# A hybrid SSD, short-convolution and mixture-of-experts block on one core: a changed gather of the second token block, a sort in another place, and changed first and last stages

## The chip, the core and the metric

The kernel runs on one core of a Trainium2 chip. Five engines work side by side, each through its own instructions in order: TensorE (PE, its weight loads PEld), VectorE (DVE), ScalarE (ACT), GpSimd (POOL) and SyncE (SP), which here issues nearly all DMAs. The metric is the device time of one execution in microseconds; the kernel before takes 448.89 us (median of 3 runs, 448.59 to 450.16).

## What is computed

One block of a decoder over 16 meta tokens and 256 tokens of width 1024, all in float32:

```python
u = rmsnorm(h, norm_mix)
proj = u @ w_in                                   # 1024 x 6160
y_ssd = ssd_branch(...)                           # Mamba-2 chunked scan
y_sc  = short_conv_branch(...)                    # gated short convolution
h = h + concatenate([y_ssd, y_sc]) @ w_out        # 2048 x 1024
u2 = rmsnorm(h, norm_ffn)
h = h + hier_moe(u2, ...)                         # 4 groups x 4 experts: best group, best 2 in it
return rmsnorm(h, norm_final)[:, N_META:]

def hier_moe(...):
    for e in range(16):
        out = out + combine[:, e:e + 1] * ((silu(t @ w_gate[e]) * (t @ w_up[e])) @ w_down[e])
```

`combine` is zero for all but two experts of a token, so only routed rows have to be multiplied.

## The kernel before

**Staging.** The order of the work is written out by hand: every engine runs its instructions in the order of the code. The weights stream through a ring of 22 slots of 1 MB (three more late in the program): `load` issues a slot's DMA on SP when the slot's last user is done, 24 tiles of `w_in`, 8 of `w_out`, 96 of the experts. The small parameter DMAs stand in a list `between`; `load` issues three of them after each piece of the first weight tiles (L95 to L97). SP's DMAs use eight completion semaphores in turn, so a DMA's issue waits for the DMA eight before it.

**The start (L697 to L730).** Tokens come in two blocks b of 128. Each is normalised: ACT sums squares (`u_squares`, in halves of 512), DVE scales by the root and by `norm_mix` (`u_scale`, L247), which a DMA has copied to all 128 partitions (`gmix`, L173); PE turns it (`u_turn`, L279) into `uh`, its low part goes to `ul`. `x_part` (L271) multiplies the identity by x, which puts the residual x into the four PSUM accumulators `acc[b][n]`. Then 48 units of 128 output columns are projected (L337, `p_dt`, `p_B`, `p_C`, ...): ACT and DVE or POOL split a weight tile into a high and a low part (`split_hi` L313, `split_lo` L324), and PE makes three products of eight matmuls.

**The routing (L900 to L974).** For each block: h out of the accumulators, its root (`h_scale`, L801), router logits, places of each token in its experts (`places`, `ranks`, `pick`). `gather` (L891) picks the tokens of unit 0, the first two experts, by multiplying h (float32) by a 0/1 matrix P into `xp`, block 0 and then block 1, and DVE scales this to `X` (`rows`, L1078). `sort_experts` (L868 to L886, 15 small DVE operations) orders the ten experts from number 6 on by their counts and leaves `order` and the largest count `mosti`.

**The experts (L1179 on).** Seven units: six of two experts with 64 token places each, and a last one of four with 32. Each: gate and up products (`gu`, L1038), the places' transposes and weights (`back`, `ptp`), the next unit's tokens from three bf16 parts of h, `hparts` (`gather3`, L1111; the parts are made at L1096 to L1104), `turned`, the down product (`yd`) in two halves of 512 columns, and the weighted sum back into the accumulators (`weighed`, `scatter` L1059). Ahead of the units stands

```python
rv = nc.values_load(mosti[0:1], min_val=0, max_val=2 * S)      # L1172
```

which every engine runs as a TENSOR_LOAD at that place of its queue (for the branch at L1292); SP also loads `order`, for the addresses of the experts from number 6 on.

**The end (L1193 to L1202, L1241 to L1290).** During the last unit `norm_final` is spread over the partitions with a diagonal matrix and `fin_part` (L1066). The last unit's result goes to the accumulators in parts, and `last_norm` squares, takes roots, scales and writes out.

Of the kernel before, what the change touches and what calls it, by code (L numbers as in the profile page):

```python
# [25 lines left out]
HALVES = [(0, 512), (512, 512)]  # L26
DUM = 5
# [11 lines left out]
def body(ctx, tc, x, meta_tokens, norm_mix, w_in, ssd_conv_w, ssd_conv_b, dt_bias, A_log, D_skip,  # L39
# [95 lines left out]
    fcol = cp.tile([128, KT], F32, name="fcol")  # L135
# [17 lines left out]
    gmix = sA[:, 0:1024]  # L153
# [32 lines left out]
    between += [(dtb[:16], raw(dt_bias, 0, [[1, 16], [1, 1]])), (alog, raw(A_log, 0, [[0, 128], [1, 16]])),
                (dsk, raw(D_skip, 0, [[1, 2], [2, 8]])), (gf, raw(norm_ffn, 0, [[KT, 128], [1, KT]])),
                (fcol, raw(norm_final, 0, [[KT, 128], [1, KT]])),
# [11 lines left out]
    A.activation(warm, eps, AF.Sqrt)  # L200
    G.iota(half[:2], pattern=[[1, 128]], base=64, channel_multiplier=-64, allow_small_or_imprecise_dtypes=True)
# [4 lines left out]
    V.memset(zero, 0.0)  # L206
# [16 lines left out]
    sup = bp.tile([128, 128], BF, name="sup")
    V.tensor_scalar(sup, jp, 0.0, None, op0=OP.is_gt)
# [6 lines left out]

    def u_squares(b):
        un[b] = un01[:, 1024 * b:1024 * b + 1024]
        for n in range(2):
            c = slice(512 * n, 512 * n + 512)
            A.activation(un[b][:, c], xt[:, b, c], AF.Square, accum_out=norms[:, 3 * n + b:3 * n + b + 1])

    def u_root(b):
        rr[b] = r = norms[:, b:b + 1]
        V.tensor_scalar(r, r, 1.0 / D, EPS, op0=OP.mult, op1=OP.add)  # L240
        A.activation(r, norms[:, 3 + b:4 + b], AF.Sqrt, bias=r, scale=1.0 / D)
# [459 lines left out]
    V.tensor_copy(f0, zero.to_broadcast([128, 2048]))  # L701
    V.tensor_add(stack, idt[:32, 0:16], idt[:32, 16:32])
# [12 lines left out]
    u_root(1)  # L715
    for q in range(2):
        t[0, q] = u_turn(0, q)
    x_part(1, 0)
# [12 lines left out]
    for i, (name, j, c, t0) in enumerate(units):  # L731
# [105 lines left out]
    def ranks(b):  # L837
# [50 lines left out]
    def gather(b, q, p, i0=0, i1=4):  # L888

        for i in range(i0, i1):  # L890
            T.matmul(p[:, i], hh[:, b].rearrange("p (m k) -> p k m", k=KT)[:, 4 * q + i],  # L891
                     P[:, b], start=(b == 0 and i == 0), stop=(b == 1),
                     skip_group_check=True)
# [57 lines left out]
    P = bp.tile([128, 2, 128], F32, name="P")  # L951
# [19 lines left out]
    sort_experts(rp[:, 96:112])  # L971
    for q in range(2):
        gather(1, q, xp[q])
# [88 lines left out]
    def fin_part(q, tag):  # L1062

        p = bank(tag, "fp")
        for i in range(4):
            T.matmul(p[:, 128 * i:128 * i + 128], on1, dg[:, 4 * q + i], start=True, stop=True)  # L1066
        V.tensor_copy(fin.rearrange("p (m k) -> p k m", k=KT)[:, 4 * q:4 * q + 4],
                      p.rearrange("p (k m) -> p k m", k=4))

# [11 lines left out]
    h3 = wk.tile([128, 2, D], BF, name="h3")  # L1081
# [11 lines left out]
    hb0, hb1 = (hh[:, b].bitcast(BF).rearrange("p (j d) -> p j d", j=2) for b in range(2))
    hparts = [[h3[:, 0], hb0[:, 0]], [h3[:, 1], hb0[:, 1]], [hb1[:, 0], hb1[:, 1]]]
    rem = [wk.tile([128, 512], F32R, name="rem", tag=t).bitcast(BF) for t in ("Yh", "Yl")]
    for b in range(2):  # L1096
        A.activation(hparts[0][b], hh[:, b], AF.Copy)
        if b == 0:
            A.activation(ws0, eps, AF.Silu)
        V.tensor_tensor(hh[:, b], hh[:, b], hparts[0][b], op=OP.subtract)  # L1100
        A.activation(hparts[1][b], hh[:, b], AF.Copy)
        V.tensor_tensor(rem[b], hh[:, b], hparts[1][b], op=OP.subtract)
    for b in range(2):
        A.activation(hparts[2][b], rem[b], AF.Copy)  # L1104
# [74 lines left out]
    for u, ne in enumerate(UNITS):  # L1179
        last = u == len(UNITS) - 1  # L1180
        Xf = X.rearrange("p k t -> p (k t)")
        for kind in range(2):
# [7 lines left out]
            if kind == 0:  # L1190
                hb = wk.tile([128, 512], F32, name="hb", tag="Yh")
                A.activation(hb, g, AF.Silu)  # L1192
                if last:  # L1193
                    ff = slot("fin", free.pop(0))
                    dg, fin = ff[:, 0:1024].rearrange("p (k m) -> p k m", k=KT), ff[:, 1024:2048]
                    oo = slot("o", free.pop(0)).rearrange("p (b d) -> p b d", b=2)
                    on1 = oo[:, 0, 0:128]
                    V.memset(on1, 1.0)
                    V.tensor_tensor(dg, idt[:, None].to_broadcast([128, KT, 128]),
                                    fcol[:, :, None].to_broadcast([128, KT, 128]), op=OP.mult)  # L1200
                    left[1, 1] = [lambda: fin_part(0, "pj")]
                    left[1, 3] = [lambda: fin_part(1, "m")]  # L1202
# [11 lines left out]
        if not last:  # L1214
# [26 lines left out]
    Y0 = [wk.tile([128, 512], F32R, name=n, tag=n) for n in ("Yh", "Yl")]  # L1241
    Y1 = ff[:, 0:512]
    A.activation(Y0[0], ys[0], AF.Copy, scale=ws)
    V.scalar_tensor_tensor(Y0[1], ys[0], ws, Y0[0].bitcast(F32), op0=OP.mult, op1=OP.subtract)
    for n in range(2):
        A.activation(Y1[:, 256 * n:256 * n + 256], ys[1][:, 256 * n:256 * n + 256], AF.Copy, scale=ws)
    for b in range(2):
        scatter(b, 0, PT, Y0[0:1])
    for b in range(2):
        for c in range(2):  # L1250
            T.matmul(acc[b][1][:, 256 * c:256 * c + 256], PT.bitcast(F32)[:, 128 * b:128 * (b + 1)],
                     Y1[:, 256 * c:256 * c + 256], start=False, stop=True, skip_group_check=True)
            if b == 0:
                scatter(c, 0, PT, Y0[1:], True)

    def norm_part(b, c0, w):
        c = slice(c0, c0 + w)
        V.scalar_tensor_tensor(oo[:, b, c], acc[b][c0 // 512][:, c0 % 512:c0 % 512 + w], s3[:, b:b + 1], fin[:, c],
                               op0=OP.mult, op1=OP.mult)
        (A if c0 == 512 else nc.sync).dma_start(raw(out, b * 128 * D + c0, [[D, 128], [1, w]]), oo[:, b, c])  # L1260

    def squares_of(b, n):
        A.activation(oo[:, b, 512 * n:512 * n + 512], acc[b][n], AF.Square, accum_out=s4[:, b, n:n + 1])
# [7 lines left out]
    def last_norm():  # L1271
        squares_of(0, 0)
        first_sum(0)
        squares_of(0, 1)
        root(0)
        V.reciprocal(s3[:, 0:1], s3[:, 0:1])
        for n in range(2):
            squares_of(1, n)

        norm_part(0, 0, 256)  # L1280
        first_sum(1)
        root(1)
# [35 lines left out]
```

## Time and profile before

| what | us |
|---|---|
| median of 3 runs (range) | 448.89 (448.59 to 450.16) |
| the profiled execution | 448.21 |
| its span in the trace | 446.2 |
| PE, DVE, ACT, POOL busy | 422.9, 229.9, 159.4, 66.2 |
| DMA: bytes moved, mean rate | 139.85 MB, 313 GB/s |

The span is what the trace covers, and 2.0 us of the profiled time lie around it. Busy time of PE counts pipelined matmuls by modelled ends, so where an engine waits says more than its share. A chain of waits is read from the last instruction backwards: each piece is what released the next.

### The profile page before, as it was taken

The numbers are of one execution on the slowest core, as the hardware profiler recorded it, in microseconds if no ns is written. First come the engines' busy times: TensorE is split into PE (matmuls) and PEld (weight loads), VectorE is DVE, ScalarE is ACT, GpSimd is POOL, SyncE is SP. The second block draws the span as 40 slices with busy tenths as digits, with TensorE's granted clock in tenths as the row PEclk, the third lists the DMA queues.
The fourth block names the chain that finished last, engine by engine and source line by source line (L and its number), as shares of the span: only waits on it lengthen the run. The fifth ranks groups of instructions, "written<-read, shape, count | busy, mean of one in ns | idle before, by whom it ended". The sixth has DMA issues, their size and how long they took to land.

```text
span 446.2 us, 7338 instructions
## 1 busy us (share of the span) xinstructions
PE 422.9 (95%) x2905; PEld 295.3 (66%) x2905; DVE 229.9 (52%) x472; ACT 159.4 (36%) x252; POOL 66.2 (15%) x39
## 2 busy tenths in 40 slices
PE   6999999999998999999999989999999999999982
PEld 4899899999997899978878353533535335353321
DVE  5679888977896858676556621110212102122113
ACT  4675446745757345554452321010010100101113
POOL 1253324244437242100000000000000000000000
PEclk9999999999999999999999999999999999999998
DMA  7999988265699556599684799999999999999952
GB/s 201 256 272 348 348 260 291 89 188 162 208 390 385 178 189 222 182 424 387 200 298 175 309 419 413 419 419 420 418 422 416 421 419 419 420 416 421 411 202 98
DMA packets 49468, 139.85 MB, mean 313 GB/s; under 512 B 6406, under 2 KB 32918, under 8 KB 37398
## 3 DMA queue, kind: packets, MB, share of 16 engines
q1 hardware_dynamic: 49142, 138.94, 82.9%
q8 instruction: 25, 0.41, 0.4%
q10 hardware_dynamic: 288, 0.39, 0.2%
q14 instruction: 13, 0.11, 0.1%
HBM read 138.26 MB, written 1.06 MB: 312 GB/s over the span
## 4 chain that ended last, share of the span: by engine, by line
PE 75%; DVE 14%; ACT 3%; SPq 3%; DMA 2%; issue 1%; ACTq 0%; DVEq 0%
PE gu L1038 22%; PE yd L1038 11%; PE acc L345 10%; PE p_c L337 5%; PE xp L1111 4%; PE p_xs L337 3%; PE p_h L337 3%; PE acc L1059 3%; PE p_z L337 3%; PE p_b L337 3%; DVE cv L593 2%; DVE h L617 2%; DVE f L324 1%; SPq L96 1%; DMA w<-in_w_in 1%
## 5 line engine op out<-in xcount | busy, mean ns | idle before, releaser
L1038 PE MATMUL gu<-w,X 128*64 128x512 f32 (+1 forms) x512 | 100.4, 595 | 0.4 <-DVE X L1078 0.4
L313 ACT ACTIVATE f<-w 128x1024 fp32r<-128x1024 f32 x64 | 67.2, 1054 | 30.8 <-PE acc L345 13.0
L324 POOL TENSOR_TENSOR f<-w,f 128x1024 fp32r<-128x1024 f32 x24 | 60.0, 2501 | 110.1 <-ACT f L313 93.6
L1038 PEld LDWEIGHTS gu<-w,X 128*64 128x64 f32 (+1 forms) x512 | 31.1, 130 | 60.2 <-issue 58.0
L324 DVE TENSOR_TENSOR f<-w,f 128x1024 fp32r<-128x1024 f32 x40 | 50.9, 1273 | 14.7 <-ACT f L313 14.6
L1038 PE MATMUL yd<-w,hd 128*64 128x512 f32 (+1 forms) x256 | 49.6, 595 | 0.5 <-DVE hd L1048 0.5
L345 PE MATMUL acc<-f,h 128*128 128x512 f32 x192 | 44.8, 391 | 0.0
L345 PEld LDWEIGHTS acc<-f,h 128*128 128x128 f32 x192 | 35.5, 188 | 7.7 <-issue 0.4
L1208 DVE TENSOR_TENSOR hb<-hb,gu 128x512 f32<-128x512 f32 x7 | 4.8, 687 | 64.3 <-PE gu L1038 62.2
L1054 DVE SCALAR_TENSOR_TENSOR Yl<-yd,ws,Yh 128x512 fp32r<-128x512 f32 x12 | 9.0, 751 | 53.6 <-PE yd L1038 38.5
L1038 PEld LDWEIGHTS yd<-w,hd 128*64 128x64 f32 (+1 forms) x256 | 15.2, 130 | 29.2 <-issue 27.6
L1053 ACT ACTIVATE Yh<-yd,ws 128x512 fp32r<-128x512 f32 x12 | 8.3, 688 | 73.4 <-PE yd L1038 56.7
L337 PE MATMUL p_b<-uh,f 128*128 128x256 f32 x128 | 16.6, 282 | 2.6 <-DVE h L605 1.9
L1111 PEld LDWEIGHTS <-hh 128*128 128x128 bf16 x192 | 18.1, 147 | 1.6 <-issue 1.6
L1111 PE MATMUL xp<-P,hh 128*128 128x128 bf16 x192 | 19.0, 225 | 0.0
L1111 PE MATMUL xp<-P,h 128*128 128x128 bf16 x96 | 16.9, 228 | 1.7 <-ACT hb L1192 1.7
L337 PE MATMUL p_xs<-uh,f 128*128 128x272 f32 x128 | 18.0, 293 | 0.1
L337 PE MATMUL p_c<-uh,f 128*128 128x258 f32 x128 | 16.9, 284 | 1.1 <-DVE h L605 1.1
L337 PEld LDWEIGHTS p_b<-uh,f 128*128 128x128 f32 x128 | 15.6, 188 | 3.4 <-issue 3.0
L1030 ACT ACTIVATE PT<-ptp 128x256 fp32r<-128x256 f32 x7 | 2.7, 384 | 42.2 <-PE ptp L1026 42.2
L1192 ACT ACTIVATE hb<-gu 128x512 f32<-128x512 f32 x7 | 4.2, 594 | 37.0 <-PE gu L1038 37.0
L337 PE MATMUL p_h<-uh,f 128*128 128x258 f32 x128 | 16.9, 285 | 0.0
(332 smaller groups left out, 664.3 us busy)
## 6 DMA issues: line engine op xcount, KB each, us to landing
w<-in_expert_w_gate SPq DMA_DIRECT2D x32, 1024.0 KB, 12.1
w<-in_expert_w_up SPq DMA_DIRECT2D x32, 1024.0 KB, 14.2
w<-in_expert_w_down SPq DMA_DIRECT2D x28, 1024.0 KB, 12.0
w<-in_w_in SPq DMA_DIRECT2D x23, 1024.0 KB, 7.3
w<-in_w_out SPq DMA_DIRECT2D x8, 1024.0 KB, 11.4
abc<-adr SPq DMA_DIRECT2D x2, 1024.0 KB, 5.7
w<-in_expert_w_down SPq DMA_DIRECT2D x4, 512.0 KB, 16.2
w<-in_expert_w_down SPq DMA_DIRECT2D x8, 256.0 KB, 6.3
```

Source lines behind the costliest of these rows:

```text
L313: A.activation(h, src, AF.Copy)
L324: (G if on_pool(name, c) else V).tensor_tensor(l, src, h.bitcast(F32), op=OP.subtract)
L337: T.matmul(p, st_[:, k, :], mv[:, k, t0:], start=(k == 0 and st_ is terms[0][0] and mv is uh), stop=(k == KT - 1 and mv is ul))
L345: T.matmul(acc[b][n], st_[:, 128 * b:128 * (b + 1)], mv[:, 512 * n:512 * (n + 1)], start=False, stop=False, skip_group_check=True)
L593: V.scalar_tensor_tensor(s[:, lo:], p[:, o - sh + lo:o - sh + n], cw[:, 3 - sh, ft:ft + 1], s[:, lo:], op0=OP.mult, op1=OP.add)
L617: V.scalar_tensor_tensor(y, cc[:, c, 2 - sh:258 - sh], scw[:, 2 - sh, t:t + 1], y, op0=OP.mult, op1=OP.add)
L1038: T.matmul(o[c * s:c * s + c], X[:, 128 * k + c * s:128 * k + c * s + c], ws_, start=first_, stop=last_, tile_position=(0, c * s))
L1053: A.activation(Yh, y, AF.Copy, scale=ws)
L1054: V.scalar_tensor_tensor(Yl, y, ws, Yh.bitcast(F32), op0=OP.mult, op1=OP.subtract)
L1059: T.matmul(acc[b][n], PT[:, 128 * b:128 * (b + 1)], part, start=False, stop=stop and part is Y[-1], skip_group_check=True)
L1111: T.matmul(p[:, i], hparts[j][b].rearrange("p (m k) -> p k m", k=KT)[:, 4 * q + i], P[:, b], start=(j == b == 0), stop=(j == 2 and b == 1))
L1208: V.tensor_mul(hb, hb, g)
```

## The change

Three places are changed.

At the start: x comes in two DMAs of 512 KB instead of four; `norm_mix` comes as 128 x 8 values on ACT's DMA queue, and is spread over the partitions on the chip (`g_spread`: a diagonal on DVE, two matmuls with ones on PE, read by `u_scale` from PSUM) instead of by the 512 KB copy; two of the four `x_part` go behind the units `p_dt` and the first `p_B`; the zeroing of `f0` goes to POOL; the small parameter DMAs are issued at other places of the weight stream.

In the routing: block 1 is split into three bf16 parts at once (`h3`, `rem1`) and gathered from these; block 0 is gathered first and as before. The three parts of block 0 are made behind `rows`, and `sort_experts` stands behind those.

At the end: `norm_final` is copied to all partitions by a DMA that SP issues ahead of its load of the count, so `fin_part` and its diagonal go; the last down product runs in pieces of 512, 256 and 256 columns, the first of them scattered and squared while the others are multiplied; `last_norm` works in halves of 512, written out from ACT's queue.

```diff
@@ load: the small DMAs between the weight tiles
-                    for a in between[:3]:
+                    few = {(0, 1): 2, (1, 0): 6}.get((j, i), 2 * (j > 5))
+                    for a in between[:few]:
                         nc.sync.dma_start(*a)
-                    del between[:3]
+                    del between[:few]
...
     nc.sync.dma_start(mt, raw(meta_tokens, 0, [[128, 128], [1, 128]]))
+    A.dma_start(gcol, raw(norm_mix, 0, [[KT, 128], [1, KT]]))
+    A.dma_start(gmt, raw(norm_mix, 0, [[0, 16], [128, 8], [1, 128]]))
     for b in range(2):
-        for n in range(2):
-            nc.sync.dma_start(xt[:, b, 512 * n:512 * n + 512], raw(x, 128 * D * b + 512 * n, [[D, 128], [1, 512]]))
-        if b == 0:
-            nc.sync.dma_start(gmt, raw(norm_mix, 0, [[0, 16], [128, 8], [1, 128]]))
-            nc.sync.dma_start(gmix, raw(norm_mix, 0, [[0, 128], [1, D]]))
+        nc.sync.dma_start(xt[:, b], raw(x, 128 * D * b, [[D, 128], [1, D]]))
...
+    def g_spread():
+
+        V.tensor_tensor(gdiag.rearrange("p (m k) -> p m k", k=KT), idt[:, :, None].to_broadcast([128, 128, KT]),
+                        gcol[:, None].to_broadcast([128, 128, KT]), op=OP.mult)
+        for n in range(2):
+            T.matmul(gp[n], all1, gdiag[:, 512 * n:512 * n + 512], start=True, stop=True)
+
+    gp = acc[0][1], acc[1][0]
...
-            V.scalar_tensor_tensor(un[b][:, c], xt[:, b, c], rr[b], gmix[:, c], op0=OP.mult, op1=OP.mult)
+            V.scalar_tensor_tensor(un[b][:, c], xt[:, b, c], rr[b], gp[n], op0=OP.mult, op1=OP.mult)
...
-    V.tensor_copy(f0, zero.to_broadcast([128, 2048]))
...
     m_sums()
+    g_spread()
     x_part(0, 0)
+    m_scale()
     u_squares(0)
     u_root(0)
-    m_scale()
-    x_part(0, 1, 0, 256)
+    u_squares(1)
+    u_root(1)
...
     mp = m_turn()
-    x_part(0, 1, 256, 512)
     u_scale(0)
     m_low(mp)
-    u_squares(1)
-    u_root(1)
     for q in range(2):
         t[0, q] = u_turn(0, q)
-    x_part(1, 0)
     x_part(1, 1)
     u_scale(1)
...
             p = project(i)
             split_lo(i + 2)
+            if i in (0, 1):
+                x_part(i, 1 - i)
...
-    gather(0, 0, xp[0])
+    gather(0, 0, xp[0], 0, 3)
     for i in range(4):
         places(1, i)
-    gather(0, 1, xp[1], 0, 1)
     ranks(1)
-    gather(0, 1, xp[1], 1, 4)
-    pick(P, 0, 1)
+
+    P1 = bp.tile([128, 2, 128], BF, name="P1")
+    A.activation(h3[:, 0], hh[:, 1], AF.Copy)
+    V.tensor_tensor(hh[:, 1], hh[:, 1], h3[:, 0], op=OP.subtract)
+    A.activation(h3[:, 1], hh[:, 1], AF.Copy)
+    V.scalar_tensor_tensor(rk[:, 1, 0:NE], mem[:, 1], -1024.0, rp[:, 80:96], op0=OP.mult, op1=OP.add)
+    pick(P1, 0, 1)
+    V.tensor_tensor(rem1, hh[:, 1], h3[:, 1], op=OP.subtract)
+    gather(0, 0, xp[0], 3, 4)
+    gather(0, 1, xp[1])
...
-    sort_experts(rp[:, 96:112])
-    for q in range(2):
-        gather(1, q, xp[q])
+    for js in ((0, 1), (2,)):
+        for k in range(KT):
+            for j in js:
+                T.matmul(xp[k // 4][:, k % 4], (h3[:, 0], h3[:, 1], rem1)[j].rearrange("p (m k) -> p k m", k=KT)[:, k],
+                         P1[:, 1], start=False, stop=(j == 2), skip_group_check=True)
...
+    fin = wk.tile([128, D], F32, name="fin")
+    nc.sync.dma_start(fin, raw(norm_final, 0, [[0, 128], [1, D]]))
...
     for q in range(2):
         rows(X, xp[q], q)
+
+    hb0, hb1 = (hh[:, b].bitcast(BF).rearrange("p (j d) -> p j d", j=2) for b in range(2))
+    hparts = [[hb1[:, 0], h3[:, 0]], [hb1[:, 1], h3[:, 1]], [hb0[:, 0], rem1]]
+    rem = wk.tile([128, 512], F32R, name="rem", tag="Yh").bitcast(BF)
+    A.activation(hparts[0][0], hh[:, 0], AF.Copy)
+    V.tensor_tensor(hh[:, 0], hh[:, 0], hparts[0][0], op=OP.subtract)
+    A.activation(hparts[1][0], hh[:, 0], AF.Copy)
+    V.tensor_tensor(rem, hh[:, 0], hparts[1][0], op=OP.subtract)
+    A.activation(hparts[2][0], rem, AF.Copy)
+    sort_experts(rp[:, 96:112], sorting)
     weights(tm)
...
-                    left[1, 1] = [lambda: fin_part(0, "pj")]
-                    left[1, 3] = [lambda: fin_part(1, "m")]
...
+    for i, tag in enumerate(("m", "m", "pj")):
+        c, n = THIRDS[i]
+        y = bank(tag, "yd")[:, :n]
+        for k in range(4):
+            side_by_side(y, hd, w_of(u, 2, k, c, n), k, k == 0, k == 3)
+        if i == 0:
+            weighed(y, ws, Y)
+        elif i == 1:
+            A.activation(Y1[:, 0:256], y, AF.Copy, scale=ws)
+            for part in Y:
+                for b in range(2):
+                    scatter(b, 0, PT, [part], part is Y[1])
+            for b in range(2):
+                squares_of(b, 0)
+        else:
+            V.tensor_scalar(Y1[:, 256:512], y, ws, None, op0=OP.mult)
...
     def last_norm():
+        for b in range(2):
+            first_sum(b)
+        for b in range(2):
+            squares_of(b, 1)
+            root(b)
+        for b in range(2):
+            V.reciprocal(s3[:, b:b + 1], s3[:, b:b + 1])
+            for n in range(2):
+                c = slice(512 * n, 512 * n + 512)
+                V.scalar_tensor_tensor(oo[:, b, c], acc[b][n], s3[:, b:b + 1], fin[:, c], op0=OP.mult, op1=OP.mult)
+                A.dma_start(raw(out, b * 128 * D + 512 * n, [[D, 128], [1, 512]]), oo[:, b, c])
```

DVE, from the ranks of block 1 (`mem` marks a token's experts) to the weights of the experts (`tm`). Before:

```order
L834 SCALAR_TENSOR_TENSOR mem<-cnt 128x16
L843 SCALAR_TENSOR_TENSOR rk<-mem,rp 128x16
L853 TENSOR_TENSOR P<-sl,rk 128x128
L868 SCALAR_TENSOR_TENSOR place<-rp,count_78 128x10
L869 TENSOR_TENSOR chain<-place 128x100
L871 TENSOR_REDUCE place<-chain 128x10
...
L886 TENSOR_TENSOR mosti<-most,srt 128x1
L1078 TENSOR_TENSOR X<-xp,gf 128x512 x2
L991 TENSOR_REDUCE tm<-lg 128x10
```

After:

```order
L842 SCALAR_TENSOR_TENSOR mem<-cnt 128x16
L971 TENSOR_TENSOR hh<-hh,h_82 128x1024
L973 SCALAR_TENSOR_TENSOR rk<-mem,rp 128x16
L862 TENSOR_TENSOR P_2610<-sl,rk 128x128
L975 TENSOR_TENSOR rem_83<-hh,h_82 128x1024
L1086 TENSOR_TENSOR X<-xp,gf 128x512 x2
L1101 TENSOR_TENSOR hh<-hh 128x1024
L1103 TENSOR_TENSOR rem<-hh 128x1024
L876 SCALAR_TENSOR_TENSOR place<-rp,count_78 128x10
L877 TENSOR_TENSOR chain<-place 128x100
...
L894 TENSOR_TENSOR mosti<-most,sorting 128x1
L1007 TENSOR_REDUCE tm<-lg 128x10
```

The sort (from `place` to `mosti`) stood ahead of `X`; it now stands behind `X` and behind two subtractions on 128 x 1024 elements, and two more such subtractions stand ahead of `X` (`h_82` is `h3`, `rem_83` is `rem1`).

PE, from the end of the gather of unit 0 to its first gate products. Before:

```order
L891 MATMUL xp<-P,hh 128x128 x3
L968 LDWEIGHTS onesb
L968 MATMUL rp<-mem,onesb 128x16
L968 LDWEIGHTS onesb
L968 MATMUL rp<-mem,onesb 128x16
L891 MATMUL xp<-P,hh 128x128 x8
L1172 TENSOR_LOAD mosti
L1038 MATMUL gu<-w_1757,X 64x512
L1038 MATMUL gu<-w_1823,X 64x512
```

After:

```order
L982 LDWEIGHTS onesb
L982 MATMUL rp<-mem,onesb 128x16
L988 LDWEIGHTS h_82
L988 MATMUL xp<-P_2610,h_82 128x128
L988 LDWEIGHTS h_82
L988 MATMUL xp<-P_2610,h_82 128x128
...
L988 LDWEIGHTS rem_83
L988 MATMUL xp<-P_2610,rem_83 128x128
...
L1179 TENSOR_LOAD mosti
L1054 MATMUL gu<-w_1754,X 64x512
L1054 MATMUL gu<-w_1820,X 64x512
```

The load of the count stands between the gather and the first `gu` in both; ahead of it are 24 matmuls with bf16 weights (`h`, then `rem`) where there were 8 with float32 weights.

PE, from the sums of the meta tokens to the first projections (`up` are the transposes, `acc_68` to `acc_71` the accumulators). Before:

```order
L251 MATMUL acc_71<-norms,sA 128x1
L271 MATMUL acc_68<-xt,idt 128x512
L271 MATMUL acc_69<-xt,idt 128x256
L261 MATMUL acc_71<-idt,sA 128x128
L271 MATMUL acc_69<-xt,idt 128x256
L279 MATMUL up<-idt,un 128x128 x8
L271 MATMUL acc_70<-xt,idt 128x512
L271 MATMUL acc_71<-xt,idt 128x512
L279 MATMUL up<-idt,un 128x128 x8
L337 MATMUL p_dt_264<-uh,f_155 128x272 x8
L337 MATMUL p_dt_264<-ul,f_155 128x272 x8
L429 MATMUL prp<-idt,sB 128x128
```

After:

```order
L250 MATMUL acc_71<-norms,sA 128x1
L230 MATMUL acc_69<-sA 128x512
L230 MATMUL acc_70<-sA 128x512
L270 MATMUL acc_68<-xt,idt 128x512
L260 MATMUL acc_71<-idt,sA 128x128
L278 MATMUL up<-idt,un 128x128 x8
L270 MATMUL acc_71<-xt,idt 128x512
L278 MATMUL up<-idt,un 128x128 x8
L336 MATMUL p_dt_259<-uh,f_138 128x272 x8
L336 MATMUL p_dt_259<-ul,f_138 128x272 x8
L270 MATMUL acc_69<-xt,idt 128x512
L428 MATMUL prp<-idt,sB 128x128
```

Two matmuls with the diagonal come in ahead, one `x_part` goes from before the transposes to behind `p_dt`, and another (`acc_70`) to behind `p_B`.

## Rows read from the trace of the kernel before

**Rows 1.** The page: transfer rate by slice, the chain by engine

```profile
GB/s 201 256 272 348 348 260 291 89 188 162 208 390 385 178 189 222 182 424 387 200 298 175 309 419 413 419 419 420 418 422 416 421 419 419 420 416 421 411 202 98
...
PE 75%; DVE 14%; ACT 3%; SPq 3%; DMA 2%; issue 1%; ACTq 0%; DVEq 0%
```

**Rows 2.** The chain of waits, 234 to 262 us: start, us, what

```profile
238.85 0.18 DVE place L868
...
242.23 0.16 DVE mosti L886
242.39 0.61 DVE X L1078
...
243.13 13.95 PE gu L1038 x64
...
257.54 1.04 ACT hh L1104
...
259.12 1.63 PE xp L1111 x24
```

**Rows 3.** The timeline, 226 to 246 us: start, us, work, idle before

```profile
232.10 2.35 ACT L801 ACTIVATE hh<-hh,rsh 128x1024 f32<-128x1024 f32 x2
...
238.67 4.07 PE L891 MATMUL xp<-P,hh 128*128 128x128 f32 x16
```

**Rows 4.** Loads of the count: ns three times, start

```profile
L1172 PEldq TENSOR_LOAD <-mosti x1: 489/489/489, 242.4 to 242.4; - x1
...
L1172 ACTq TENSOR_LOAD <-mosti x1: 472/472/472, 256.6 to 256.6; - x1
```

**Rows 5.** The timeline, 246 to 275 us

```profile
248.28 1.22 DVE L1100 TENSOR_TENSOR hh<-hh,h 128x1024 f32<-128x1024 f32 x1
...
249.53 1.06 ACT L1101 ACTIVATE h<-hh 128x1024 bf16<-128x1024 f32 x1 [2.87 <-DVE hh L1100]
```

**Rows 6.** Windows at the start: busy by engine, clock, DMA share, GB/s

```profile
8.00:10.00 2.00, 0.18 (x1) 0.18 (x2) 0.98 (x2) 0.46 (x1) 0.00 (x0) 0.86 1.20 284
10.00:12.00 2.00, 2.00 (x9) 1.92 (x10) 1.10 (x5) 1.76 (x7) 0.00 (x0) 0.50 0.73 172
12.00:14.00 2.00, 2.00 (x5) 0.73 (x4) 2.00 (x5) 0.69 (x3) 0.00 (x0) 0.78 0.70 176
```

**Rows 7.** The timeline, 0 to 36 us

```profile
9.02 1.42 DVE L247 SCALAR_TENSOR_TENSOR un<-xt,norms,sA 128x512 f32<-128x512 f32 x2 [2.11 <-DMA sA<-in_norm_mix]
...
9.82 1.97 PE L279 MATMUL up<-idt,un 128*128 128x128 f32 x8 [2.11 <-DVE un L247]
...
11.58 2.52 PE L271 MATMUL acc<-xt,idt 128*128 128x512 f32 x4
...
15.23 1.28 PE L337 MATMUL p_dt<-uh,f 128*128 128x272 f32 x8 [0.25 <-ACT uh L280]
```

**Rows 8.** The chain over the whole span, units 0 and 1

```profile
271.50 1.12 PE acc L1059 x4
...
275.61 10.45 PE gu L1038 x48
286.44 1.63 PE xp L1111 x24
```

**Rows 9.** The timeline, 404 to 446 us

```profile
417.55 1.16 PE L1066 MATMUL fp<-fin,o 128*128 128x128 f32 x8
...
427.68 7.07 PE L1038 MATMUL yd<-w,hd 128*32 128x512 f32 x64 [0.52 <-DVE hd L1048]
...
438.46 0.58 ACT L1263 ACTIVATE o<-acc 128x512 f32<-128x512 f32 x1
...
439.92 1.53 DVE L1258 SCALAR_TENSOR_TENSOR o<-acc,s,fin 128x512 f32<-128x512 f32 x3
```

**Rows 10.** The same windows at the end

```profile
428.00:430.00 2.00, 2.00 (x24) 0.65 (x20) 0.00 (x0) 0.00 (x0) 0.00 (x0) 1.00 0.82 298
430.00:436.00 6.00, 5.97 (x53) 1.99 (x42) 0.75 (x1) 1.53 (x3) 0.00 (x0) 1.00 0.03 12
```

More of the change, by code (lines that the diff above doesn't have):

```diff
@@ L26 @@
 HALVES = [(0, 512), (512, 512)]
+THIRDS = [(0, 512), (512, 256), (768, 256)]
 DUM = 5
@@ L182, in body @@
     row = lambda p, n: raw(p, 0, [[128, n], [1, 128]])
+    between += [(dtb[:16], raw(dt_bias, 0, [[1, 16], [1, 1]])), (alog, raw(A_log, 0, [[0, 128], [1, 16]]))]
     between += [(pr[a:a + n, :], row(p, n)) for p, a, n in (
@@ L185, in body @@
         (norm_ffn, 120, 8))]
[L186 to L188 removed]
+    between += [(dsk, raw(D_skip, 0, [[1, 2], [2, 8]])), (gf, raw(norm_ffn, 0, [[KT, 128], [1, KT]])),
                 (wgr, raw(router_group_w, 0, [[4, 128], [512, KT], [1, 4]])),
@@ L200, in body @@
     A.activation(warm, eps, AF.Sqrt)
+    V.memset(zero, 0.0)
+    f0 = slot("f0").bitcast(F32R)
+    G.memset(all1, 1.0)
+    G.tensor_copy(f0[:, 0:1024], zero.to_broadcast([128, 1024]))
     G.iota(half[:2], pattern=[[1, 128]], base=64, channel_multiplier=-64, allow_small_or_imprecise_dtypes=True)
@@ L230, in body @@
     un01 = slot("un")
+    def g_spread():
[4 more added lines that the diff above has]
+    gp = acc[0][1], acc[1][0]
     def u_squares(b):
         un[b] = un01[:, 1024 * b:1024 * b + 1024]
-        for n in range(2):
-            c = slice(512 * n, 512 * n + 512)
-            A.activation(un[b][:, c], xt[:, b, c], AF.Square, accum_out=norms[:, 3 * n + b:3 * n + b + 1])
+        A.activation(un[b], xt[:, b], AF.Square, accum_out=norms[:, 3 + b:4 + b])
     def u_root(b):
         rr[b] = r = norms[:, b:b + 1]
-        V.tensor_scalar(r, r, 1.0 / D, EPS, op0=OP.mult, op1=OP.add)
-        A.activation(r, norms[:, 3 + b:4 + b], AF.Sqrt, bias=r, scale=1.0 / D)
+        A.activation(r, norms[:, 3 + b:4 + b], AF.Sqrt, bias=eps, scale=1.0 / D)
     def u_scale(b):
@@ L891, in gather @@
             T.matmul(p[:, i], hh[:, b].rearrange("p (m k) -> p k m", k=KT)[:, 4 * q + i],
-                     P[:, b], start=(b == 0 and i == 0), stop=(b == 1),
-                     skip_group_check=True)
+                     P[:, b], start=(i == 0), stop=False, skip_group_check=True)
     def busy(n):
@@ L950, in body @@
     busy(1)
-    P = bp.tile([128, 2, 128], F32, name="P")
+    P = bp.tile([128, 1, 128], F32, name="P")
     pick(P, 0, 0)
@@ L1060, in scatter @@
                      stop=stop and part is Y[-1], skip_group_check=True)
[L1062 to L1068, printed above, removed]
     def w_of(u, kind, k, c, n):
@@ L1090, in body @@
         pick(P, 0, b)
[L1093 to L1104, printed above, removed]
     def gather3(P, X, q):
@@ L1219, in body @@
             P = Pn
+        if last:
+            break
         ys = [bank("m", "yd") for n in range(2)]
@@ L1238, in body, with squares_of @@
         left[0, 3] = [lambda b=b, PT=PT, k=keep: scatter(b, 1, PT, k[0]) for b in range(2)]
[L1241 to L1248, printed above, removed]
+    oo = slot("o", free.pop(0)).rearrange("p (b d) -> p b d", b=2)
+    Y1 = wk.tile([128, 512], F32, name="Y1", tag="X")
+    Y = [wk.tile([128, 512], F32R, name="Yh", tag="Yh"), slot("Y", free.pop(0)).bitcast(F32R)[:, 0:512]]
+    def squares_of(b, n):
+        A.activation(oo[:, b, 512 * n:512 * n + 512], acc[b][n], AF.Square, accum_out=s4[:, b, n:n + 1])
+    for i, tag in enumerate(("m", "m", "pj")):
+        c, n = THIRDS[i]
+        y = bank(tag, "yd")[:, :n]
+        for k in range(4):
+            side_by_side(y, hd, w_of(u, 2, k, c, n), k, k == 0, k == 3)
+        if i == 0:
[9 more added lines that the diff above has]
+            V.tensor_scalar(Y1[:, 256:512], y, ws, None, op0=OP.mult)
+    used(2 * ne)
     for b in range(2):
@@ L1252, in body @@
                      Y1[:, 256 * c:256 * c + 256], start=False, stop=True, skip_group_check=True)
[L1253 to L1263, printed above, removed]
     def first_sum(b):
@@ L1271, in last_norm @@
     def last_norm():
[L1272 to L1282, printed above, removed]
-        norm_part(0, 256, 256)
-        norm_part(0, 512, 512)
-        V.reciprocal(s3[:, 1:2], s3[:, 1:2])
-        norm_part(1, 0, 512)
-        norm_part(1, 512, 256)
-        norm_part(1, 768, 256)
+        for b in range(2):
[9 more added lines that the diff above has]
+                A.dma_start(raw(out, b * 128 * D + 512 * n, [[D, 128], [1, 512]]), oo[:, b, c])
     last_norm()
@@ L1293, in body @@
         over()
+        for b in range(2):
+            squares_of(b, 0)
         last_norm()
```

46 lines of the change are left out of this document (17 added, 29 removed).

## The prediction

> **What bounds the kernel now.** I read the page first. The chain that ended last is PE for 75% of the span, DVE for 14%, SP and DMA for 5% [rows 1]. The reader is to see in the transfer rates that from the 24th slice on (256 us) the DMA moves some 419 GB/s in every slice to 424 us, while the 21st to the 23rd, around the routing, lie at 298, 175 and 309 [rows 1]. So the second half of the kernel has two tracks of nearly equal length, PE's and the DMA's, and both start from the first gate product, because that product's use of the first tiles is what frees ring slots. Then I read the chain of waits through the routing, the timeline there, at the start and at the end, and the granted clock in windows.
>
> In the chain around 239 us [rows 2] DVE is the carrier: the sort runs from 238.85 to 242.39, X is written at 242.39 to 243.0, and PE's first gate product begins at 243.13. The gather of block 1 that runs beside the sort takes PE 4.07 us from 238.67 [rows 3], so it too ends just ahead of X: neither alone is worth much.
>
> **The routing: what becomes earlier.** The 16 passes in float32 (4.07 us) are replaced by 24 matmuls on bf16 parts. The expert stage has just such 24 in 1.63 us, 0.068 each [rows 2], so PE would be done at 238.85 + 1.63 = 240.5. The parts must be there: ACT ends the scaling at 234.45 [rows 3]; copy 1.06, subtract 1.22, copy 1.06, subtract 1.22 (an operation of each kind is in [rows 5]) give 239.2 with hand-overs and the wait for DVE's ranking, and the third part is wanted at 238.85 + 16 x 0.068 = 239.9. So PE is not held up, and X, two DVE operations of 0.61 from 240.3 on, stands at 241.6, where it stood at 243.6: 2.0 us earlier. If the parts came later, X would lose up to this gain.
>
> **The routing: what becomes later.** PE loads `mosti` into a register at its place in the queue, between the gather and the gate products. In the trace this load began at 242.4, as soon as the count was written, and took 0.49 us; ACT's, whose condition was met at the same time, ran at 256.6, when its turn came behind the copies of h [rows 4]. So a load waits both for the count and for its place, and I take it that what stands behind it waits too. Before, this costs nothing: the count is done at 242.39, the load at 242.9, X's first half at 243.0.
>
> Behind the change the count comes last. From X at 241.6: subtract 1.22, ACT's copy 1.06, subtract 1.22 [rows 5], and then the 15 operations of the sort, 242.39 - 238.85 = 3.54 [rows 2]; with 0.1 of hand-overs 248.7. From the count to the first gate product it was 243.13 - 242.39 = 0.74, which the load and its hand-over may fill; so 249.45 instead of 243.13, **6.3 us later**. On DVE the expert weights (`tm`) and the picks queue behind the sort; they have the 14 us of the gate and up products as cover. SP's load of the count is late as well, but the first slot is freed only 3.5 us into the gate products.
>
> PE then stands idle from 240.5 to 249.4. [...] The work lost there is 2 x (0.14 + 0.50 + 0.22) = 1.7 us. [...]
>
> So PE's and DMA's tracks through the experts both start 8.0 us later.
>
> **The start.** DVE waits 2.11 us for the copied `norm_mix` before it scales block 0 at 9.02, and PE waits 2.11 for that [rows 7]. With the diagonal (one DVE operation on 128 x 1024, 1.22 as in [rows 5]) and two products on a cold PE, four passes of 0.63 as in the 2.52 us of the `x_part` at 11.58 [rows 7], the spread stands near 7 to 8 us: I choose 3 us for the arrival of the 128 x 8 values, whose DMA is the first on its queue; then the diagonal at 4.3, the meta sums' matmul, and the passes to some 7.5. Block 0's scaling then ends 1.5 us earlier, block 1's 2 us, and with one `x_part` out of the way the first projection, now at 15.23 [rows 7], begins near 12.3. Since PE is nearly always busy from there to the routing, the two `x_part` now inside the stream are paid: four passes at full clock, 13.95 us / 32 = 0.44 each (64 rows, two experts side by side [rows 2]), 1.75 us. Net 2.9 - 1.75 = 1.15; the weight tiles' earlier issue may save a part of PE's later waits: I take **1.4 us** gained. Bounds: nothing (the spread is as late as the copy, or POOL's zeroing holds DVE) and 3.
>
> **Unit 0.** There PE waits from 257.08 to 259.12, 2.04 us, for ACT's late copies of h's parts [rows 2]; in unit 1 the same gap is 0.38 [rows 8]. The parts are now made ahead: **1.66 us** gained, by PE's track alone.
>
> **The end.** The two `fin_part` leave PE: 1.09 us each in the chain, 1.16 in the timeline [rows 9]; **2.2 us**, again PE's track alone. The copy that replaces them (512 KB) moves while the DMA is idle: no cost. The last down product stood at 427.68; now at 427.68 + 8.0 - 1.4 - 1.66 - 2.18 = 430.4.
>
> The DMA's track has neither gain. Its last weights landed near 429.5: 298 GB/s from 428 to 430, 12 afterwards [rows 10]; PE's last step wanted them at 433.9, the eighth of 7.07 / 8 = 0.88 us [rows 9]. Now they land at 429.5 + 8.0 - 1.4 = 436.1, and the second piece of the product (256 columns) needs them at 430.4 + 3.53 + 3 x 0.44 = 435.3. So the DMA ends the wait, by 0.8 us. From 436.1: the step 0.44, the scatter's four matmuls 1.1 [rows 8], the third piece 1.77, in all 439.4. Behind it: scaling 0.5, three products of 0.44, a square 0.58 [rows 9] and its sum, 0.8 and a root 0.3, then the reciprocal and two or three of the 512-wide scalings (1.53 for 512 + 256 + 256 [rows 9], so some 0.65), some 5.2 in all, for 6.7 before (434.75 to 441.45). That is 444.6, against 441.45: 3.15 later; the last output DMA has 256 KB instead of 128, 0.3 more.
>
> **The sum.** 448.21 (profiled) + 3.4 = 451.6. The median of the runs shown lies 0.7 above the profiled execution, which would make it 452.3; I take 452.0.
>
> **The rivals.**
> *The load does not hold PE.* The wait is then on X alone: gate products at 241.05, 2.1 earlier than now, no idle stretch. DMA's last weights at 429.5 - 2.1 - 1.4 = 426.0; by the same steps the last scaling ends at 426.0 + 8.5 = 434.5, 6.95 earlier, with 0.3 for the output 441.6 by the profile, 441.9. This is the faster side. For it: before, PE's gate products start 0.13 behind X's first half, so the trace never shows PE held. Against it: ACT's load, which kept its place for 14 us. It decides from the point where mosti is later than X. [...]
> [...]
> *Held, and more.* The start gives nothing and the slow clock lasts twice as long: 429.5 + 9.7 + 8.5 = 447.7, so 448.21 + 6.25 + 0.3 = 454.8, 455. For it: four more DVE operations of 128 x 1024 ahead of the sort, any of which may be late, and an idle stretch four times as long as at the start.
>
> **How the numbers follow.** Less than 0.5% (2.2 us, so 446.6 to 451.1) is what a measurement of this kernel can't tell from no change. The forecast has a chance of 0.60, in 450.3 to 454, of which 0.10 falls below 451.1; paid back 0.14, held and more 0.09, not held 0.17. So slower 0.59, same 0.24, faster 0.17. The range leaves out the case that PE isn't held and the far end of the third rival: 447 to 456.
>
> **What would show it.** PE's load of the count starting near 247 to 249 us, some 6 us behind X, with the first gate product right behind it; about 9 us without a matmul ahead of it, then windows with a granted clock near 0.5; X written 2 us earlier than now, relative to the ranks of block 0; a gap near 0.4 us in unit 0 between the up product and `xp`; no `fp` rows; `p_dt` near 12.3 us; the first expert loads of the loop issued some 7 us later; and in the last unit a wait of PE for a weight DMA. If the gate products start before the count is written, the forecast is wrong altogether; if the start gives some 5 us, it is wrong in sign.

## The result: slower, 454.4 us, and the profile after

The changed kernel takes 454.4 us (median of 7, 452.1 to 455.8), the kernel before 449.55 beside it: a ratio of 1.0092 (1.0067 to 1.0117). On another chip, in the experiments below, it was 454.39 again, 1.0087 (1.0056 to 1.0118). The forecast was 452.0; slower by more than the 0.5% that a measurement can tell, as it said. The profiled execution took 454.67 us with a span of 452.8 (before 448.21 and 446.2).

Page of the changed kernel, granted clock and transfer rate in 40 slices. The rates answer to [rows 1]:

```profile
PEclk9999999999998999999996899999999999999997
...
GB/s 234 343 290 270 349 261 237 68 180 208 211 411 315 114 245 209 249 419 310 200 384 61 185 428 416 423 418 420 422 421 421 418 423 418 421 420 422 410 199 96
```

Ahead of the steady rate of some 420 GB/s the 22nd and 23rd slice now have 61 and 185, where [rows 1] have 175 and 309: the pause of the DMA at the routing has grown. The clock has a small dent in the 13th slice (136 to 147 us) and a deep one in the 22nd and 23rd (238 to 260 us).

Timeline of the changed kernel through the routing (start, us, engine, line, work, idle before; in all rows a `q` behind an engine's name means its instruction queue). It answers to [rows 2, 3]:

```profile
237.23 1.23 DVE L975 TENSOR_TENSOR rem<-hh,h 128x1024 bf16<-128x1024 f32 x1 [0.71 <-ACT h L972]
239.44 1.29 DVE L1086 TENSOR_TENSOR X<-xp,gf 128x512 f32<-128x512 f32 x2 [0.98 <-PE xp L988]
...
244.12 0.16 DVE L876 SCALAR_TENSOR_TENSOR place<-rp,count 128x10 f32<-128x10 f32 x1
...
247.48 0.16 DVE L894 TENSOR_TENSOR mosti<-most,sorting 128x1 int32<-128x1 f32 x1
...
248.35 0.32 PEld L1054 LDWEIGHTS gu<-w,X 128*64 128x64 f32 x4 [8.86 <-DVE tm L1011]
248.38 15.62 PE L1054 MATMUL gu<-w,X 128*64 128x512 f32 x64 [8.75 <-DVE tm L1011]
```

The row of X before, in the same view (the chain of [rows 2] has it from 242.39 on, when the count is done):

```profile
242.31 1.28 DVE L1078 TENSOR_TENSOR X<-xp,gf 128x512 f32<-128x512 f32 x2
```

X starts at 239.44, where it stood at 242.31; the count at 247.48, where it stood at 242.23; PE idles for 8.75 us and starts its gate products at 248.38 instead of 243.13. The profile puts the wait down to VectorE's work on `tm` at 248.14. That is only the event that came last: the gate product reads neither `tm` nor anything made from it. The row to read is that of the register load, grouped by line as in [rows 4]:

```profile
L1179 PEldq TENSOR_LOAD <-mosti x1: 489/489/489, 247.7 to 247.7; - x1
...
L1179 DVEq TENSOR_LOAD <-mosti x1: 546/546/546, 251.8 to 251.8; - x1
```

PE's load starts as soon as the count is there (247.7), ends at 248.2, and weights and products follow. VectorE's own load has its turn only at 251.8, behind the weights and the picks in its queue.

Windows of the changed kernel behind it (busy time of PE, PEld, DVE, ACT, POOL, then clock, DMA share, GB/s), as in [rows 6]:

```profile
240.00:242.00 2.00, 0.00 (x0) 0.00 (x0) 1.85 (x3) 0.11 (x1) 0.00 (x0) 0.89 0.62 186
...
246.00:248.00 2.00, 0.00 (x0) 0.00 (x0) 1.83 (x11) 0.00 (x0) 0.00 (x0) 0.50 0.00 0
248.00:250.00 2.00, 1.62 (x4) 0.59 (x6) 1.62 (x11) 1.72 (x3) 0.00 (x0) 0.50 0.04 8
250.00:252.00 2.00, 2.00 (x8) 0.69 (x6) 1.76 (x8) 0.00 (x0) 0.00 (x0) 0.55 0.00 0
```

The products start at half clock (0.50 in the windows from 246 to 250 us, 0.55 in the next), and the gate and up product of unit 0 takes 15.62 us instead of 13.95.

The start and, between 132 and 146 us, what became of its gain; PE's timeline of the changed kernel, then two of its windows:

```profile
11.29 1.24 PE L336 MATMUL p_dt<-uh,f 128*128 128x272 f32 x8 [0.25 <-ACT uh L279]
...
15.63 0.30 PE L428 MATMUL prp<-idt,sB 128*128 128x128 f32 x1 [1.02 <-DMA sB<-in_norm_ffn]
...
43.43 2.25 PE L336 MATMUL p_xs<-uh,f 128*128 128x272 f32 x16
...
138.49 3.23 PE L336 MATMUL p_b<-uh,f 128*128 128x256 f32 x16 [1.95 <-DVE h L604]
```

```profile
138.00:140.00 2.00, 1.51 (x9) 1.54 (x10) 0.67 (x3) 1.56 (x3) 1.27 (x2) 0.79 1.02 408
140.00:142.00 2.00, 2.00 (x12) 2.00 (x11) 0.00 (x0) 1.98 (x3) 2.00 (x1) 0.50 1.01 403
142.00:144.00 2.00, 2.00 (x18) 1.46 (x18) 0.42 (x1) 0.63 (x2) 0.26 (x1) 0.86 0.10 39
```

The first projection starts 3.94 us earlier than in [rows 7]; two `x_part` in the stream (1.02 us each) and a new wait of 1.02 us for the DMA of `norm_ffn` take most of that back, and with some shorter waits behind them 1.74 is left at 43 us (45.17 before). At 138 us the clock falls to 0.50 behind a wait of 1.95 us. The profiled execution of before has the same wait (1.92 us) and keeps 1.00; its rows of PE, then its windows:

```profile
45.17 2.27 PE L337 MATMUL p_xs<-uh,f 128*128 128x272 f32 x16
...
140.28 2.12 PE L337 MATMUL p_b<-uh,f 128*128 128x256 f32 x16 [1.92 <-DVE h L605]
```

```profile
138.00:140.00 2.00, 0.36 (x4) 0.15 (x2) 2.00 (x2) 0.00 (x0) 2.00 (x2) 1.00 1.03 408
140.00:142.00 2.00, 1.72 (x15) 1.75 (x15) 0.47 (x2) 1.77 (x4) 1.27 (x2) 1.00 1.02 410
```

The end: timeline of the changed kernel, then its windows and those of before in which the last bytes move ([rows 9, 10]):

```profile
437.96 0.62 PE L1054 MATMUL yd<-w,hd 128*32 128x256 f32 x2 [0.39 <-SPq L1289]
...
444.15 1.41 DVE L1284 SCALAR_TENSOR_TENSOR o<-acc,s,fin 128x512 f32<-128x512 f32 x2
...
444.94 3.97 ACTq L1285 DMA_DIRECT2D out<-o  x4
...
445.67 1.41 DVE L1284 SCALAR_TENSOR_TENSOR o<-acc,s,fin 128x512 f32<-128x512 f32 x2
```

```profile
437.30:437.40 0.10, 0.10 (x2) 0.00 (x0) 0.10 (x1) 0.00 (x0) 0.00 (x0) 1.00 0.05 20
437.40:437.50 0.10, 0.10 (x1) 0.00 (x0) 0.04 (x1) 0.00 (x0) 0.00 (x0) 1.00 0.01 0
```

```profile
430.80:430.90 0.10, 0.10 (x8) 0.04 (x4) 0.00 (x0) 0.00 (x0) 0.00 (x0) 1.00 0.12 41
430.90:431.00 0.10, 0.10 (x4) 0.00 (x0) 0.00 (x0) 0.00 (x0) 0.00 (x0) 1.00 0.01 0
```

In windows of 0.1 us the transfers end near 437.4 (before near 430.9); the step that needs them runs at 437.96, and the last scaling ends at 447.08 (before 441.45).

### The profile page after: what moved, and what is told of

It reads as the page before. It is cut to its first block, busy times and chain, and to the rows that moved or that the text cites. A ratio compares the mean times of both kernels' runs of the same rounds, so it can differ in the third digit from the quotient of the medians.

```text
span 452.8 us, 7374 instructions
## 1 busy us (share of the span) xinstructions
PE 423.9 (94%) x2931; PEld 292.8 (65%) x2931; DVE 226.7 (50%) x465; ACT 158.0 (35%) x246; POOL 67.8 (15%) x41
## 5 line engine op out<-in xcount | busy, mean ns | idle before, releaser
L1054 PE MATMUL gu<-w,X 128*64 128x512 f32 (+1 forms) x512 | 101.7, 602 | 8.7 <-DVE tm L1011 8.7
L1054 PE MATMUL yd<-w,hd 128*64 128x512 f32 (+2 forms) x288 | 52.1, 548 | 0.9 <-DVE hd L1064 0.5
L1054 PEld LDWEIGHTS yd<-w,hd 128*64 128x64 f32 (+1 forms) x288 | 16.9, 128 | 30.7 <-issue 24.9
L336 PE MATMUL p_b<-uh,f 128*128 128x256 f32 x128 | 17.7, 294 | 2.8 <-DVE h L604 1.9
L336 PEld LDWEIGHTS p_b<-uh,f 128*128 128x128 f32 x128 | 16.6, 200 | 3.6 <-issue 3.2
L336 PE MATMUL p_z<-uh,f 128*128 128x256 f32 x128 | 16.8, 284 | 0.0
L336 PEld LDWEIGHTS p_xs<-uh,f 128*128 128x128 f32 x128 | 16.4, 188 | 0.6 <-issue 0.5
```

The source lines that it names most:

```text
L336: T.matmul(p, st_[:, k, :], mv[:, k, t0:], start=(k == 0 and st_ is terms[0][0] and mv is uh), stop=(k == KT - 1 and mv is ul))
L1054: T.matmul(o[c * s:c * s + c], X[:, 128 * k + c * s:128 * k + c * s + c], ws_, start=first_, stop=last_, tile_position=(0, c * s))
```

## Experiments

Ratios are to the kernel before on the same chip; its median there was 450.24 us for e1_late_read, e2_sort_ahead, m_alone and e_alone, 449.1 for s_alone, warm_gap, sm_late and late_fill, and 450.13 for warm_full, after_again, before_late and late_again.

**The count read late (e1_late_read).**

```diff
-    rv = nc.values_load(mosti[0:1], ...)         # ahead of the unit loop, as is SP's read of order
+        if u == 2:                               # inside the unit loop
+            rv = nc.values_load(mosti[0:1], ...)
+                if place >= FIXED and not chosen:  # in load(): SP's read, where first needed
+                    read_order()
```

> The changed kernel, but the count's read into a register stands in unit 2 instead of ahead of the gate products, and SP reads the sorted experts only ahead of the first load that needs one. The sort keeps its place behind X and the copies of h. Theory (the read holds PE): the first gate product starts 0.7 us behind the start of X, near 240.2 us instead of 248.38, with no idle stretch of more than 1.5 us ahead of it; with PE not idle the clock's loss of 1.67 us goes as well, so both tracks start 9.8 us earlier and the time is 454.4 - 9.8 = 444.6 us (443 to 447). Rival (the read holds nothing; PE waits for the weights' chain on VectorE, which the profile names beside the idle time, or for another product of it): the gate product still starts near 248 us and the time stays at 454 us. Third case (PE is freed, but SP or the picks hold the tracks): gate product at 240, first expert load of the loop later than 247 us, time 448 to 451.

443.85 us, 0.9862 (0.983 to 0.9895). PE's timeline, then rows of VectorE and SP:

```profile
239.39 13.10 PE L1061 MATMUL gu<-w,X 128*64 128x512 f32 x60 [0.54 <-DVE X L1093]
```

```profile
238.65 1.29 DVE L1093 TENSOR_TENSOR X<-xp,gf 128x512 f32<-128x512 f32 x2 [0.99 <-PE xp L995]
...
243.07 0.80 SPq L120 DMA_DIRECT2D w<-in_expert_w_gate  x2
...
243.33 0.16 DVE L883 SCALAR_TENSOR_TENSOR place<-rp,count 128x10 f32<-128x10 f32 x1
```

The gate products run 4 us before the sort of the counts has even begun, 0.74 us behind the start of X (238.65). The rival falls: without the read in front, PE waits for X alone. Nor does the third case hold, since SP's first expert load is issued at 243.07 (253.72 in the changed kernel, 246.78 before). SP's read, which the edit moved as well, held nothing beyond PE: that load follows the first gate product by 3.7 us here and in the kernel before, and by 5.3 in the changed kernel, where the product runs 1.67 slower.

**The sort ahead of X (e2_sort_ahead).**

```diff
+    sort_experts(rp[:, 96:112], sorting)
     for q in range(2):
         rows(X, xp[q], q)
     ...
-    sort_experts(rp[:, 96:112], sorting)
```

> The changed kernel with the sort moved back ahead of X alone; the read stays where it is. Theory (the read holds PE until the count): sort 238.4 to 242.0 us, X 242.0 to 243.2, the read at 242.0 to 242.5 is done before X's first half, the gate product starts near 242.7 us, 5.7 earlier than in the changed kernel; the idle stretch is 3 us instead of 8.75, and of the 1.67 us lost to the clock between none and all comes back: 447.0 to 448.7, I take 448. Rival (the place of the sort is not what costs): 453 to 455 us.

448.36 us, 0.9958 (0.9931 to 0.9985). Its read and its first gate product:

```profile
L1179 PEldq TENSOR_LOAD <-mosti x1: 490/490/490, 241.6 to 241.6; - x1
```

```profile
242.29 10.09 PE L1054 MATMUL gu<-w,X 128*64 128x512 f32 x46 [3.00 <-DMA fin<-in_norm_final]
```

As expected: 6.1 us earlier than in the changed kernel, from one moved line. The idle stretch of 3.00 us did not drop the clock in the profiled execution (446.48 us), which has 1.00 in all windows from 238 to 254 us; the other executions lie between 444.94 at a mean clock of 0.993 and 450.84 at 0.983.

**The three parts alone (m_alone, e_alone, s_alone).** Each is the kernel before with one part of the diff and nothing of the other two.

> The kernel before with the edits of the middle alone (8-bit parts for the second half, sort behind X and the copies of h); start and end as before. Theory (all of the loss comes from here): first gate product 5.95 us later than before, near 249.1 us, 1.67 us more lost to the clock, unit 0's gap 1.66 shorter; at the end PE's track is the longer one (last product 433.6 us), so + 6.0: 455.5 us (454 to 457). Rival (the loss is in the end, the middle gives back what it takes): 449 to 452 us.

> The kernel before with the edits of the end alone (last down product in three pieces, fin by DMA, one shared tail). Theory (a small gain): the last weights land as before at 429.5 us, the last product starts 2.2 us earlier, the tail behind the last weights is 10.6 us as in the changed kernel instead of 11.95, and the last output transfer is 1.0 us longer: 449.55 - 1.35 + 1.0 = 449.2 us (448 to 450.5). Rival (the new end is itself slower, and explains what the forecast lacked): 451.5 us or more.

> The kernel before with the edits of the start alone; middle and end as before. Theory: by 43 us the changed kernel is 1.74 us ahead of before (p_xs at 43.43 instead of 45.17) and still 1.79 ahead at 130.7 us; only a dip of the granted clock to 0.50 behind PE's 1.95 us wait for p_b at 136.5 us, which the profiled execution of before lacks, takes 1.1 us of it. So the start is worth 1.75 us against executions of before that dip as often: 450.24 - 1.75 = 448.5 us. Rival (the start's gain is really lost on the way to the routing, as 0.69 there says): 449.5 us.

Middle (the "8-bit parts" are the bf16 parts of the diff): 457.63 us, 1.0168 (1.0133 to 1.0203), so the loss does come from there; 2.1 us more than expected, and above the range.

```profile
251.39 15.70 PE L1048 MATMUL gu<-w,X 128*64 128x512 f32 x64 [8.99 <-DVE tm L1005]
```

The wait (8.99) and the slow product (15.70) are those of the changed kernel; but in this execution the routing itself came 2.1 us later than before: 1.4 by the same dip of the clock at 142 us (0.58 and 0.57 in two windows), and 0.7 that stand at 133 us already. At that place the profiled executions with the old start scatter: 132.1 us in e_alone, 132.5 in the kernel before, 133.2 here, 133.4 in before_late.

End: 448.47 us, 0.9964 (0.9942 to 0.9986); a gain of 1.6 us by the ratio (0.6 to 2.6), where the expectation's sum had 0.35. Start: 447.27 us, 0.9953 (0.9936 to 0.997), a gain of 2.1 us (1.3 to 2.9), so the rival (0.7) falls. The product of the three ratios is 1.0084, against 1.0092 and 1.0087 for the whole: the parts add up.

**PE kept busy while it waits (warm_gap, warm_full).**

```diff
+    dmy = bank("pj", "dmy")
+    for i in range(30):                          # 37 in warm_full
+        T.matmul(dmy[:, 0:128], idt, idt, start=True, stop=True)
     rv = nc.values_load(mosti[0:1], min_val=0, max_val=2 * S)
```

> The changed kernel with 30 more matmuls of the identity with itself, into a PSUM bank that nobody reads, between the gather and the count's read: PE is busy for 7.6 of the 8.75 us in which it stood idle, and still waits for the count. Theory (the slower gate and up product of unit 0, 15.62 us instead of 13.95, is the clock): the first gate product starts as in the changed kernel, near 248.4 us, the granted clock stays at 1.00 to 254 us, and the time falls by 1.67: 452.7 us. Rival (the clock is not what makes it slow, or DMA's track hides it): 454 to 455 us.

454.37 us, 1.0114 (1.0088 to 1.0139): no gain, though the profiled execution, at 452.79 the lowest, shows just what was expected (product 13.96 us, clock 1.00). The 30 matmuls took 6.92 us and left 2.00 idle, and the five other executions had mean clocks of 0.986 to 0.990 against 0.993. That the clock fell in those 2.00 us is not shown: a dip like that at 138 us alone, 2 x (0.21 + 0.50 + 0.14) = 1.7 us, takes 0.004 off the mean. In the next run the gap was closed:

> The changed kernel with 37 instead of 30 matmuls into the unread bank, at 0.231 us each 8.5 us, so that no idle stretch of 2 us is left ahead of the first gate product. Theory (the clock costs 1.67 us behind the held read, and with 30 matmuls the 2.0 us that stayed idle dropped it in most executions, though not in the profiled one): gate product near 248.2 us, clock 1.00 to 254 us, 1.7 us below the changed kernel on the same chip, ratio to before 1.0055, mean clock of the executions 0.992 or more. Rival (the clock there costs the total nothing, because DMA ends the waits later): as the changed kernel on the same chip, within 0.6 us.

> The changed kernel once more, on the chip on which the next three run: 1.009 of before (1.007 to 1.012).

warm_full: 452.71 us, 1.0064 (1.0039 to 1.009), mean clocks of 0.990 to 0.995; the changed kernel beside it 454.39, mean clocks of 0.978 to 0.985 (its idle stretch at 0.50 counts in them). The difference of the medians is 1.68 us, the expected size; the two intervals overlap, so the size is not sharper than that. PE's timeline and a window of warm_full:

```profile
237.83 8.48 PE L1181 MATMUL dmy<-idt 128*128 128x128 f32 x74
246.74 3.65 PE L1054 MATMUL gu<-w,X 128*64 128x512 f32 x16 [0.43 <-DVE tm L1011]
```

```profile
246.00:248.00 2.00, 1.57 (x9) 0.69 (x10) 1.62 (x12) 1.60 (x3) 0.00 (x0) 1.00 0.00 0
```

Even with PE busy up to 0.43 us before, the product starts no sooner: 10.43 us behind the first matmul on the bf16 parts (236.31), where after_again, idle there, has 10.40 (238.75 to 249.15). Useful work in the gap was not tried; that it would not move that start either is an estimate from these two.

**The late read in the kernel before (before_late)**, with the edit of e1_late_read:

> The kernel before with the late read (count read in unit 2, sorted experts read ahead of the first load that needs one), nothing else. Theory (there the read was done at 242.9 us, before X's first half at 243.0, so it held nothing): ratio 1.000, within 0.5 us of before, gate product 0.1 to 0.4 us behind X as now. Rival (the read itself or SP's read costs, apart from the count's lateness): 0.5 to 1 us faster than before.

450.69 us, 1.0004 (0.9981 to 1.0027), the gate product waits 0.31 us for X, and for nothing else. The same instruction that costs 10 us behind the change cost nothing before it.

**The old end with the late read (sm_late)**: the late read with the start and the middle of the change, and the end of before.

> The kernel with the late read (443.85 us), but with the end as it was before the change. Theory (the effects add up; the end alone gave 450.24 - 448.47 = 1.8 us): 443.85 + 1.8 = 445.6 us, with the last scaling 1.8 us later. Rival (where the DMA's last weights end the wait, the new end gains nothing or costs its longer last transfer): 443.0 to 443.9 us.

444.14 us, 0.9881 (0.9856 to 0.9906), beside 0.9862 and 0.9857 with the new end: 0.3 us slower by the medians, some 1 by the ratios, against the theory's 1.8, with intervals that overlap. The size of the end's gain here stays open; it is likely smaller than alone.

**The wait at 137 us filled (late_fill).**

```diff
+            if name == "b0" and c == 2:
+                dmy = bank("m", "dmy")
+                for q in range(7):
+                    T.matmul(dmy[:, 0:128], idt, idt, start=True, stop=True)
             p = project(i)
```

> The kernel with the late read (443.85 us), and 7 matmuls of the identity with itself, into a PSUM bank that nobody reads, ahead of the third p_b projection, where PE otherwise waits 1.9 us near 137 us. Theory (that wait trips the clock in a part of the executions, at 1.1 us each): no dip in 130 to 150 us, the median 0.5 to 1.1 us lower, 442.8 to 443.4 us, and the mean clock of each execution higher and more alike. Rival (the dip has another cause, or what it takes is hidden): 443.9 us, with the same scatter.

443.46 us, 0.9872 (0.9846 to 0.9898), so no gain against before that e1_late_read (0.9862) has not. The profiled execution shows no dip, but neither do those of e1_late_read and of the run below, so this run can't tell what the dip costs a median. Inconclusive.

The traces of all runs tell what it costs one execution. Thirteen of them have that wait, of 1.89 to 1.95 us. In seven (both of the changed kernel, e2_sort_ahead, sm_late and the three parts alone) the clock falls behind it, and from the first `p_b` to the logits it is 98.8 to 99.0 us; in the other six it is 97.4 to 97.7. So a dip costs 1.1 to 1.6 us, and the length of the wait does not tell whether it comes.

**The late read again (late_again)**, beside after_again:

> The changed kernel with the late read once more, on the same chip as the changed kernel itself: 0.986 of before (0.983 to 0.990), and 10 us below the changed kernel, of which 8.2 are the held start, 1.67 the clock behind it.

443.84 us, 0.9857 (0.9819 to 0.9895), 10.55 below the changed kernel on the same chip. It beats both kernels.

## Why the prediction was right, and where it was off

- *PE is held by the read.* Right. The first gate product came 5.25 us later by the clock and 5.94 relative to the routing, which stood 0.69 earlier; the forecast was 6.3. e1_late_read and before_late show the cause: the same read moved away gives 10 us behind the change and nothing without it. The rival "the load does not hold PE" gave 441.9 us for a kernel in which nothing is held; that kernel, built, takes 443.85. In the changed kernel's trace no weight load passed the waiting register load: the first came at 248.35, 8.86 us after the last one, though X had been written at 240.73.
- *X earlier.* 2.0 us forecast, 2.87 by the clock, 2.18 relative to the routing.
- *The cold clock.* The forecast's 8.0 us for both tracks are 6.3 and 1.7 for the clock, an estimate from what the three windows of [rows 6] lack to 1.00; no run of the kernel before shows such a loss at the routing. The runs behind the change show 1.67 in the product's length, 1.68 between the medians of warm_full and the changed kernel; 15.56 and 15.70 us for the product in the traces of after_again and m_alone say the same. Behind the wait the granted clock was 0.50 from 248 to 250 us, 0.55 to 252 and 1.00 after that.
- *Unit 0 and `fin_part`.* The gap ahead of `xp` is some 0.3 us for 2.04, and no `fp` is left; the last down product starts at 430.51, forecast 430.4. It gave no time, as the forecast had it: the DMA ended the wait.
- *The start.* 1.4 us forecast for the routing, 0.69 in the profiled execution. The start itself gives more, not less: 1.74 at 43 us, 2.1 by s_alone. The 3 us for the arrival of the `norm_mix` values were the author's choice; the diagonal that reads them starts at 2.62. `p_dt` came 1.0 ahead of the forecast's 12.3, and the 1.02 us for `norm_ffn`, which the forecast did not have, took that back. What is missing at the routing is the dip at 138 us, in a wait that both kernels have: from `p_b` at 130.69 to the logits at 229.46 it is 98.77 us, where the five profiled executions with the changed start and no dip take 97.4. Without those 1.35 us the routing would stand 2.0 earlier.
- *The end: the step that failed.* "Its last weights landed near 429.5" read the end of a 2 us window; by windows of 0.1 us the transfers go on to 430.9, and in the changed kernel to 437.4, so 6.5 later than before (6.6 forecast). PE's step runs 0.56 behind that, for which the forecast had nothing. So 437.96 for 436.1: 1.86 late, of which 1.4 is this reading, −0.1 the shift and 0.56 the delay of the step. From there the tail took 9.12 us to the last scaling (8.5 forecast) and the output 5.72 behind it (4.75 before, 0.3 more forecast). 1.86 + 0.62 + 0.67 = 3.15, and 451.65 + 3.15 = 454.8, against 454.67.

So 454.4 lies within the range of 447 to 456, but above the 450.3 to 454 of the forecast case itself. That it lies by the 455 of "held, and more" is an accident of sums: the start did give its time, and the slow clock lasted as forecast.

## What to carry to other kernels

In this kernel what stood behind a register load in PE's queue waited for the load's data, needed or not: 8.75 us for the gate products. So a move of the producer must be followed to every engine that reads it, and a read for a late branch belongs where its data have long been ready. When an idle engine is named as waiting for work whose result it doesn't use, look for such a load. Read the end of a transfer in narrow windows and add the time until the waiting matmul starts; here those two made 2.0 of the 3.15 us by which the end came late.

## Not expected of the hardware

- Idle stretches of like length did and did not drop the granted clock: 1.89 to 1.95 us near 137 us did in seven of thirteen profiled executions (1.95 in the changed kernel, not 1.92 in the kernel before), and 3.00 us near 240 us did not in e2_sort_ahead's. What decides is not shown; executions whose code is the same up to there, as those of the changed kernel and of e1_late_read, differ by it.
- From the last bytes of a transfer to the matmul that waits for them: some 0.5 us (437.4 to 437.96).
